# One body and a loop in place of seven nested bodies for the extra units of an expert layer

## The chip, the cores and the metric

The kernel runs on one core of one Trainium2 chip. The metric is device time in microseconds (us) of one execution, smaller being better; the median of several runs is compared.

## The reference, cut to what matters

An encoder of two layers over 256 tokens of width 1024. Each layer mixes tokens and then applies a mixture of 32 experts in 4 groups of 8: a token takes the group with the largest logit and in it the two experts with the largest logits.

```python
for g in range(N_EXPERT_GROUPS):
    h = jax.nn.silu(jnp.einsum('nd,edf->enf', xt, w_gate[g])) * jnp.einsum('nd,edf->enf', xt, w_up[g])
    h = h * gate[:, g].T[:, :, None].astype(h.dtype)
    y = y + jnp.einsum('enf,efd->nd', h, w_down[g])
```

`gate` is zero for all experts but a token's two. How many tokens an expert gets is known only at run time.

## The kernel before, in words

The kernel streams all weights of all 32 experts of a layer from HBM (3 MB an expert, in pages of 1 MB) through a ring of 25 pages in on-chip memory. The list of pages (`chunks`) has a fixed order; `pump` (L227) issues transfers on SyncE's queue (SP) as long as the plan says that pages are free, and each `done` and `work_done` calls it again.

`moe` (L1194) goes over the experts of a layer in nine blocks of two or four (`ORDER`). A block of four has 32 slots for an expert, one of two has 64. For a block the tokens of its experts are gathered by matmuls with a one-hot matrix (`gather`, L1232), multiplied with the gate and up weights (`gate_up`, L1442), made hidden values (`hidden`, L1345, and `hidden_t`, L1351), multiplied with the down weights (`down`, L1458), split into a high and a low part (`split_y`, L1359) and added to x (`combine`, L1251 to L1253). `fill_slots` (L1335) makes the matrix that takes slots back to tokens, by two transposes, a copy on ScalarE (L1341) and a compare on VectorE (L1342); it writes into `scr`, a work page of the ring that each block takes anew.

Where an expert of a block of four has more than 32 tokens, `second` (L1480) does the block once more for the next 32; it stands within a test (`tc.If`, L1559 and L1589). Where an expert has more than 64 tokens, each further 128 are a unit. `unit_list` (L1300) makes the list of units on VectorE: in `uw["ui"]` the expert of each unit, up to 7 (`MAXU`), and in place 14 their number; `uw["ub"]` holds the experts and the first slots as numbers on every partition. `unit_prepare` (L1374), in block 3 of layer 0 and block 4 of layer 1, takes work pages for a unit's weights and issues the five transfers of unit 0 (`unit_load`, L1366: two of gate, two of up, one of down), each with the condition that there is a unit at all.

After block 3 of layer 0 and block 5 of layer 1 (`UNIT_AT`), `unit_chain` (L1423) runs: a test for unit 0, within it the body of unit 0 and a test for unit 1, within that the loads and the body of unit 1, and so on to unit 6. A unit (`unit`, L1381) is some 25 instructions on VectorE, matmuls at L1398, L1411 and L1419, transposes, and a `combine`. Every engine makes the tests by itself, from the number of units that it reads into a register at L1606. After the units `work_done(6, 4)` gives six pages back to the ring: three of weights, one of tokens, `scr` and the block's `y`.

The framework puts each engine's instructions in order, assigns the semaphores of engines and transfers, and adds the semaphore instructions of a test that fails.

Of the kernel before, what the change touches and what calls it, by code (L numbers as in the profile page):

```python
# [14 lines left out]
I32 = mybir.dt.int32  # L15
# [43 lines left out]
MAXU = 7  # L59
# [102 lines left out]
def hybrid_encoder_kernel(ctx, tc, I, out, dbg=None):  # L162
    nc = tc.nc
    V, S, G, PE = nc.vector, nc.scalar, nc.gpsimd, nc.tensor
# [5 lines left out]
    def ps(name):  # L170
        return psp.tile([128, 512], F32, tag="ps", name=name)
# [97 lines left out]
    def work_done(n, peak=None):  # L269
        st["nw"] -= n  # L270
        if peak is not None:
            st["peak"] = peak
        pump()
# [89 lines left out]
    def either(dst, src, scale=None):  # L363

        flip[0] ^= 1
        st["bits"], st["picked"] = "SV"[flip[0]], 0
        copy(dst, src, scale)
# [3 lines left out]
    def transpose(dst, src):  # L371
        PE.transpose(dst, src, ident[:src.shape[0], :src.shape[0]])  # L372
# [4 lines left out]
    def page_sm(t, o, shape):  # L377
        n = int(np.prod(shape))
        v = t[:, o:o + n]
        if len(shape) == 2:  # L380
            v = v.rearrange("p (a b) -> p a b", a=shape[0])
        elif len(shape) == 3:
            v = v.rearrange("p (a b c) -> p a b c", a=shape[0], b=shape[1])
        return v
# [809 lines left out]
    def moe(l, tab, rt):  # L1194
        with tc.tile_pool(name=f"moe{l}", bufs=1, reuse_waits="tile") as mo:
            vc = vec[:, l, :]

            def mt(shape, name, dt=F32, tag=None, bufs=1):
                return mo.tile(shape, dt, tag=tag or name, name=name, bufs=bufs)
# [45 lines left out]
            def combine(pend, hfs=(0, 1)):  # L1245
                Sm, yh, yl = pend
                for hf in hfs:
                    for tt in range(2):
                        p = ps("cp")
                        c = slice(512 * hf, 512 * hf + 512)  # L1250
                        PE.matmul(p, Sm[:, 128 * tt:128 * tt + 128], yh[:, c], start=True, stop=False)  # L1251
                        PE.matmul(p, Sm[:, 128 * tt:128 * tt + 128], yl[:, c], start=False, stop=True)  # L1252
                        V.tensor_tensor(x[:, tt, c], p, x[:, tt, c], OP.add)  # L1253
# [76 lines left out]
            def slots(blocks, tag=""):  # L1330

                n = 1 if tag else 2
                return (mt([128, T], "sm" + tag, F32R, bufs=n), mt([128, 1], "gs" + tag, bufs=n)), blocks

            def fill_slots(arg):  # L1335
                (Sm, gs), blocks = arg
                p = ps("slp")
                for tt in range(2):
                    transpose(p[:, 128 * tt:128 * tt + 128], blocks[tt])
                gj = scr[0][:, 1024:1280]  # L1340
                S.activation(gj, p[:, :T], AF.Copy, accum_out=gs)  # L1341
                V.tensor_scalar(Sm, p[:, :T], 0.0, None, op0=OP.is_gt)  # L1342
                return Sm, gs

            def hidden(gu, gs):  # L1345
                sl, hh = scr[0][:, 1280:1536], scr[0][:, 1536:1792]
                S.activation(sl, gu[:, 0:256], AF.Silu)  # L1347
                V.scalar_tensor_tensor(hh, gu[:, 256:512], gs, sl, op0=OP.mult, op1=OP.mult)  # L1348
                return hh

            def hidden_t(hh, o=1792):  # L1351
                hp = ps("hp")
                for j in range(2):
                    transpose(hp[:, 128 * j:128 * j + 128], hh.rearrange("p (f j) -> p j f", j=2)[:, j, :])
                hT = page_sm(scr[0], o, (2, 128))
                S.copy(hT.rearrange("p a b -> p (a b)"), hp[:, :256])
                return hT

            def split_y(yp, yh, yl, c):  # L1359
                S.copy(yh[:, c], yp)  # L1360
                V.tensor_tensor(yl[:, c], yp, yh[:, c].bitcast(F32), OP.subtract)  # L1361


            uw = {}

            def unit_load(u, **kw):  # L1366
                e = nc.sync.value_load(uw["ui"][0:1, u:u + 1], min_val=0, max_val=NE - 1)
                for h in range(2):
                    for a, n in enumerate(("w_gate", "w_up")):
                        nc.sync.dma_start(uw["gu"][h][:, a], I[n][l][ds(e, 1)].rearrange(  # L1370
                            "a (p k) f -> p (a k) f", k=8)[:, 4 * h:4 * h + 4, :], **kw)
                nc.sync.dma_start(uw["dn"], I["w_down"][l][ds(e, 1)].rearrange("a (p j) d -> p (a j) d", j=2), **kw)
# [8 lines left out]
            def unit(u):  # L1381
                ub = uw["ub"]
                oh, rs_, jk = mt([128, NE], "ohu"), mt([128, 4], "rsu"), mt([128, NE], "jku")
                V.tensor_scalar(oh, io32, ub[:, u:u + 1], None, op0=OP.is_equal)
                for tt in range(2):
                    V.tensor_tensor_reduce(jk, rk[:, tt, :], oh, 1.0, 0.0, OP.mult, OP.add, rs_[:, tt:tt + 1])
                    V.tensor_tensor_reduce(jk, gate[:, tt, :], oh, 1.0, 0.0, OP.mult, OP.add, rs_[:, 2 + tt:3 + tt])
                V.tensor_scalar(rs_[:, 0:2], rs_[:, 0:2], ub[:, MAXU + u:MAXU + u + 1], None, op0=OP.subtract)
                Pu, Pg = mt([128, 2, 128], "Pu", tag="oh"), page_sm(scr[0], 1536, (2, 128))
                for tt in range(2):  # L1390
                    V.tensor_scalar(Pu[:, tt], iota, rs_[:, tt:tt + 1], None, op0=OP.is_equal)
                    V.tensor_scalar(Pg[:, tt], iota, rs_[:, tt:tt + 1], rs_[:, 2 + tt:3 + tt], op0=OP.is_equal,
                                    op1=OP.mult)
                xu, xuT = uw["xu"][:, :D], page_sm(uw["xu"], D, (8, 128))
                for hf in range(2):
                    p = ps("gpu")
                    for tt in range(2):
                        PE.matmul(p, Pu[:, tt], xn[:, tt, 4 * hf:4 * hf + 4, :].rearrange("p k d -> p (k d)"),  # L1398
                                  start=(tt == 0), stop=(tt == 1))
                    either(xu[:, 512 * hf:512 * hf + 512], p)  # L1400
                for hf in range(2):
                    p = ps("xup")
                    for k in range(4):
                        transpose(p[:, 128 * k:128 * k + 128], xu[:, 128 * (4 * hf + k):128 * (4 * hf + k) + 128])
                    V.tensor_tensor(xuT[:, 4 * hf:4 * hf + 4, :], p.rearrange("p (k s) -> p k s", k=4),
                                    vc[:, V_LN2 + 4 * hf:V_LN2 + 4 * hf + 4].unsqueeze(2).to_broadcast([128, 4, 128]),
                                    OP.mult)
                Sm, gs = fill_slots(slots([Pg[:, 0], Pg[:, 1]]))
                gu = ps("guu")
                for k in range(8):  # L1410
                    PE.matmul(gu.rearrange("p (a f) -> p a f", a=2), xuT[:, k], uw["gu"][k // 4][:, :, k % 4, :],  # L1411
                              start=(k == 0), stop=(k == 7))
                hT = hidden_t(hidden(gu, gs))
                yh, yl = uw["y"]
                for hf in range(2):
                    c = slice(512 * hf, 512 * hf + 512)
                    yp = ps("ypu")
                    for j in range(2):
                        PE.matmul(yp, hT[:, j, :], uw["dn"][:, j, c], start=(j == 0), stop=(j == 1))  # L1419
                    split_y(yp, yh, yl, c)  # L1420
                combine((Sm, yh, yl))

            def unit_chain(nu, u):  # L1423
                with tc.If(nu > u):  # L1424
                    if u:
                        unit_load(u)
                    unit(u)
                    if u + 1 < MAXU:
                        unit_chain(nu, u + 1)

            def gate_up(gu, blk, xs, hf, ahead=None):

# [72 lines left out]
            for g, grp in enumerate(groups):  # L1505
# [3 lines left out]
                for ib, b in enumerate(grp):  # L1509
# [92 lines left out]
                    if b == UNIT_AT[l]:  # L1602
                        combine(pend)
                        pend = None
                        n = 2 * MAXU
                        unit_chain(nc.values_load(uw["ui"][0:1, n:n + 1], min_val=0, max_val=MAXU), 0)  # L1606
                        work_done(6, 4)
                    if b >= TAB_AT and tab is not None:
                        next(tab, None)
# [54 lines left out]
    for l in range(L):  # L1664
        rt = mixer(l)
        if dbg and dbg.get("stop") == ("mixer", l):
            break
        moe(l, follow(l + 1, TABLES.split(), s5_steps(l + 1), STATE) if l + 1 < L else None, rt)
        if dbg and dbg.get("stop") in (("moe", l), ("blk", l)):
            break  # L1670
# [26 lines left out]
```

## Time and profile before

| | us |
|---|---|
| median of 3 runs | 740.88 (740.05 to 741.61) |
| the profiled execution | 737.13 |
| its span, first to last instruction | 735.4 |
| mean granted TensorE clock, share of full speed | 0.955 |

The profile is of one execution. Its engines are PE (TensorE's matmuls), PEld (its weight loads), DVE (VectorE), ACT (ScalarE), POOL (GpSimd) and SP (SyncE, which only issues transfers here). A q behind an engine's name marks an instruction of its sequencer: branches, semaphore instructions, issues of transfers. `L1442` is a line of the kernel. `out<-in` are names of tiles: `pg` is a page of weights, `gu` the result of gate and up, `slp` the transposed slots, `scr` the work page.

### The profile page before, as it was taken

The page shows a single profiled execution, that of the slowest core. Times are in us where ns is not written, and L with a number is a line of the kernel's source. Part 1 is how long each engine was busy: PE and PEld are TensorE (multiplying, and loading weights), DVE is VectorE, ACT ScalarE, POOL GpSimd, SP SyncE. Part 2 cuts the span into 40 slices and gives each one's busy share as a digit, 9 for nine tenths or more (in the row PEclk, how much of TensorE's full clock was granted, in tenths as well). Part 3 has the DMA queues.
Part 4 walks back from the last instruction along what each step waited for, and adds up shares of the span by engine and source line. Part 5 has one row for each costly group of instructions (what it writes and reads, how often), then busy time and mean ns, then how long its engine had stood idle before and what let it go on. Part 6 is the DMA issues. An engine that isn't in the chain of part 4 may idle for free. (4 is left out here: it accounts for less than half of the span.)

```text
span 735.4 us, 12004 instructions
## 1 busy us (share of the span) xinstructions
PE 631.6 (86%) x4370; PEld 386.3 (53%) x4370; DVE 373.7 (51%) x899; ACT 253.2 (34%) x578; POOL 107.5 (15%) x135
## 2 busy tenths in 40 slices
PE   7997989889799498598799899989899987769994
PEld 6584877744245334336268677775444434324442
DVE  3899977532334117824279878752423324322424
ACT  3647873421012014524074397352111211001113
POOL 1202001000000021521051754510000000000001
PEclk9999999999899799889999999989999999979998
DMA  8920375896999899999994715895999999998992
GB/s 304 419 108 0 117 289 215 331 389 231 413 406 416 280 405 411 412 415 407 398 417 183 286 59 172 302 362 194 333 416 406 392 410 413 416 366 301 410 382 83
DMA packets 57207, 232.90 MB, mean 317 GB/s; under 512 B 6048, under 2 KB 8480, under 8 KB 48160
## 3 DMA queue, kind: packets, MB, share of 16 engines
q1 hardware_dynamic: 57120, 231.75, 81.5%
q8 instruction: 53, 0.87, 0.5%
q14 instruction: 34, 0.28, 0.1%
HBM read 233.82 MB, written 1.05 MB: 319 GB/s over the span
## 5 line engine op out<-in xcount | busy, mean ns | idle before, releaser
L1442 PE MATMUL gu<-pg,xe 128*32 128x512 f32 (+1 forms) x1024 | 147.9, 618 | 12.4 <-DMA pg<-in_w_up_dram 7.1
L1458 PE MATMUL yp<-pg,scr 128*32 128x512 f32 (+2 forms) x560 | 79.4, 639 | 25.9 <-DVEq L1589 11.5
L1442 PEld LDWEIGHTS gu<-pg,xe 128*32 128x32 f32 (+1 forms) x1024 | 48.1, 117 | 96.7 <-issue 91.0
L1236 PE MATMUL gp<-oh,xn 128*128 128x128 f32 (+1 forms) x416 | 71.2, 325 | 4.0 <-DVE oh L1221 2.0
L1236 PEld LDWEIGHTS gp<-oh,xn 128*128 128x128 f32 x416 | 61.4, 197 | 18.6 <-issue 10.6
L1458 PEld LDWEIGHTS yp<-pg,scr 128*32 128x32 f32 (+1 forms) x560 | 22.1, 120 | 73.0 <-issue 58.2
L1361 DVE TENSOR_TENSOR y<-yp,y 128x512 fp32r<-128x512 f32 (+1 forms) x39 | 26.3, 677 | 65.8 <-ACT y L1360 65.8
L1348 DVE SCALAR_TENSOR_TENSOR scr<-gu,gs,scr 128x256 f32<-128x256 f32 x19 | 9.1, 481 | 97.1 <-ACT scr L1347 97.1
L1228 POOL TENSOR_TENSOR pgt<-oh,gate 128x256 f32<-128x256 f32 (+1 forms) x13 | 10.2, 783 | 316.5 <-PE slp L372 304.6
L1253 DVE TENSOR_TENSOR x<-cp,x 128x512 f32<-128x512 f32 x76 | 48.9, 685 | 14.2 <-PE cp L1252 14.2
L1360 ACT CAST y<-yp 128x512 fp32r<-128x512 f32 (+1 forms) x39 | 22.3, 575 | 88.1 <-PE yp L1458 86.6
L359 DVE TENSOR_SCALAR xe<-gp,vec 128x128 f32<-128x128 f32 (+1 forms) x52 | 20.8, 400 | 52.0 <-PE gp L1236 52.0
L355 ACT ACTIVATE xe<-gp,vec 128x128 f32<-128x128 f32 (+1 forms) x52 | 21.3, 409 | 73.3 <-PE gp L1236 73.2
L1347 ACT ACTIVATE scr<-gu 128x256 f32<-128x256 f32 x19 | 7.3, 384 | 102.3 <-PEq L1559 52.3
L1251 PE MATMUL cp<-y,sm 128*128 128x512 f32 x76 | 34.0, 455 | 0.3 <-PEq L1559 0.2
L1252 PE MATMUL cp<-y,sm 128*128 128x512 f32 x76 | 30.4, 409 | 1.5 <-DVE y L1361 1.5
L1058 DVE SCALAR_TENSOR_TENSOR x<-op,rg,x 128x512 f32<-128x512 f32 x24 | 17.9, 749 | 16.8 <-PE op L681 11.9
L1341 ACT ACTIVATE scr<-slp 128x256 f32<-128x256 f32 x20 | 7.8, 388 | 42.2 <-SPq L1424 28.8
L1251 PEld LDWEIGHTS cp<-y,sm 128*128 128x128 f32 x76 | 14.5, 192 | 10.4 <-issue 8.2
L372 PE MATMUL hp<-cst,scr 128*128 128x128 f32 x40 | 9.3, 314 | 12.2 <-DVE scr L1348 11.1
L372 PE MATMUL slp<-cst,pgt 128*128 128x128 f32 x36 | 8.3, 314 | 11.2 <-DVEq L1424 5.9
L1252 PEld LDWEIGHTS cp<-y,sm 128*128 128x128 f32 x76 | 14.3, 193 | 5.5 <-DVE y L1361 3.8
(454 smaller groups left out, 1209.2 us busy)
## 6 DMA issues: line engine op xcount, KB each, us to landing
pg<-in_w_gate_dram SPq DMA_DIRECT2D x128, 512.0 KB, 10.1
pg<-in_w_up_dram SPq DMA_DIRECT2D x128, 512.0 KB, 10.4
pg<-in_w_down_dram SPq DMA_DIRECT2D x56, 1024.0 KB, 11.8
pg<-in_w_o_dram SPq DMA_DIRECT2D x8, 1024.0 KB, 18.0
pg<-in_w_down_dram SPq DMA_DIRECT2D x12, 512.0 KB, 10.4
pg<-in_w_qk_dram SPq DMA_DIRECT2D x4, 1024.0 KB, 14.9
pg<-in_w_nat_dram SPq DMA_DIRECT2D x4, 960.0 KB, 12.8
wgu<-in_w_gate_dram SPq DMA_DIRECT2D x4, 512.0 KB
```

The source lines that it names most:

```text
L355: S.copy(dst, src) if scale is None else S.activation(dst, src, AF.Copy, scale=scale)
L359: e.tensor_scalar(dst, src, scale, None, op0=OP.mult)
L372: PE.transpose(dst, src, ident[:src.shape[0], :src.shape[0]])
L1058: V.scalar_tensor_tensor(xh, p, rg[:, g, tt:tt + 1], xh, op0=OP.mult, op1=OP.add)
L1236: PE.matmul(p[:, :w], xn[:, tt, k, :], P[:, tt].rearrange("p e c -> p (e c)"), start=(tt == 0), stop=(tt == 1))
L1251: PE.matmul(p, Sm[:, 128 * tt:128 * tt + 128], yh[:, c], start=True, stop=False)
L1252: PE.matmul(p, Sm[:, 128 * tt:128 * tt + 128], yl[:, c], start=False, stop=True)
L1253: V.tensor_tensor(x[:, tt, c], p, x[:, tt, c], OP.add)
L1360: S.copy(yh[:, c], yp)
L1361: V.tensor_tensor(yl[:, c], yp, yh[:, c].bitcast(F32), OP.subtract)
L1442: PE.matmul(gu[m * s:m * s + m, :].rearrange("p (a f) -> p a f", a=2), xs(k, s), page(l, "gu", e, hf)[:, :, k % 4, :], start=(k == 0), sto ...
L1458: PE.matmul(yp[m * s:m * s + m, :], hT[:, j, m * s:m * s + m], page(l, "dn", e)[:, j, c], start=(j == 0), stop=(j == 1), tile_position=(0, ...
```

## The change

`units` takes the place of `unit_chain`. Unit 0 has its body within the first test, as before. Within a test for a second unit stands a loop over units 1 to the last. Its body moves the lists of units down by one place on VectorE (six copies in all), loads the weights of what is now unit 0, and runs the body for unit 0.

```diff
-            def unit_chain(nu, u):
-                with tc.If(nu > u):
-                    if u:
-                        unit_load(u)
-                    unit(u)
-                    if u + 1 < MAXU:
-                        unit_chain(nu, u + 1)
+            def units(nu):
+
+                with tc.If(nu > 0):
+                    unit(0)
+                    with tc.If(nu > 1):
+                        with tc.For_i(1, nu, 1):
+                            ui, ub = uw["ui"], uw["ub"]
+                            for a in (0, MAXU):
+                                mv = mt([128, MAXU], "umv")
+                                V.tensor_copy(mv[:, :MAXU - 1], ub[:, a + 1:a + MAXU])
+                                V.tensor_copy(ub[:, a:a + MAXU - 1], mv[:, :MAXU - 1])
+                            mi = mt([1, MAXU], "umi", I32)
+                            V.tensor_copy(mi[:, :MAXU - 1], ui[:, 1:MAXU])
+                            V.tensor_copy(ui[:, :MAXU - 1], mi[:, :MAXU - 1])
+                            unit_load(0)
+                            unit(0)
...
-                        unit_chain(nc.values_load(uw["ui"][0:1, n:n + 1], min_val=0, max_val=MAXU), 0)
+                        units(nc.values_load(uw["ui"][0:1, n:n + 1], min_val=0, max_val=MAXU))
```

## Rows read from the trace of the kernel before

**Rows 1.** The page: its span, and the transfer rate in 40 equal slices.

```profile
span 735.4 us, 12004 instructions
...
GB/s 304 419 108 0 117 289 215 331 389 231 413 406 416 280 405 411 412 415 407 398 417 183 286 59 172 302 362 194 333 416 406 392 410 413 416 366 301 410 382 83
```

**Rows 2.** Stretches: PE, PEld, DVE, ACT, POOL busy us (instructions), clock, DMA share, GB/s.

```profile
241.00:252.00 11.00, 3.18 (x15) 2.07 (x19) 1.12 (x2) 0.48 (x2) 0.00 (x0) 0.59 0.69 219
252.00:259.00 7.00, 6.60 (x56) 4.15 (x48) 0.00 (x0) 0.27 (x1) 0.00 (x0) 0.91 1.01 346
259.00:350.00 91.00, 74.64 (x720) 39.01 (x724) 46.95 (x111) 34.99 (x68) 21.82 (x22) 0.94 1.02 412
...
657.00:664.00 7.00, 6.94 (x54) 1.85 (x45) 0.49 (x2) 0.47 (x2) 0.00 (x0) 0.82 0.44 173
664.00:673.00 9.00, 9.00 (x80) 5.44 (x84) 2.89 (x6) 1.12 (x4) 0.00 (x0) 1.00 0.91 272
```

**Rows 3.** SP's waits from 250 to 390: who <- whom, us, times, longest.

```profile
SPq L247 <- DMA pg<-in_w_down_dram: 29.3, 19, 2.2
```

**Rows 4.** Issues of transfers: times issued, KB each, median us to landing.

```profile
pg<-in_w_gate_dram SPq DMA_DIRECT2D x128, 512.0 KB, 10.1
```

**Rows 5.** Timeline at layer 0's units: start, us, instruction, [idle before <- releaser].

```profile
239.75 0.07 SPq L1372 DMA_DIRECT2D wdn<-in_w_down_dram  x1
...
243.45 0.33 SPq L247 DMA_DIRECT2D pg<-in_w_gate_dram  x1
...
244.48 0.66 PE L372 MATMUL slp<-cst,pgt 128*128 128x128 f32 x2 [5.29 <-PEq L1424]
...
248.90 0.33 SPq L247 DMA_DIRECT2D pg<-in_w_up_dram  x1
248.97 0.38 ACT L1341 ACTIVATE scr<-slp 128x256 f32<-128x256 f32 x1 [11.51 <-SPq L1424]
...
249.48 9.11 PE L1442 MATMUL gu<-pg,xe 128*32 128x512 f32 x64 [4.34 <-issue]
```

**Rows 6.** SP's waits from 243 to 249.3.

```profile
SPq L1424 <- SPq L1424: 4.6, 4, 2.7
```

**Rows 7.** The units' test: count, ns min/median/max, first to last start.

```profile
L1424 SPq EVENT_SEMAPHORE  x18: 17/17/17, 244.3 to 662.8; - x18
...
L1424 PEldq COMPARE_BRANCH  x4: 70/2794/6028, 238.7 to 653.1; - x4
```

**Rows 8.** Timeline at layer 1's units.

```profile
646.61 0.33 SPq L247 DMA_DIRECT2D pg<-in_w_gate_dram  x1
...
651.63 0.33 SPq L247 DMA_DIRECT2D pg<-in_w_up_dram  x1
...
653.59 0.66 PE L372 MATMUL slp<-cst,pgt 128*128 128x128 f32 x2 [5.95 <-DVEq L1424]
...
654.18 9.71 PE L1442 MATMUL gu<-pg,xe 128*32 128x512 f32 x64
...
662.97 0.39 ACT L1341 ACTIVATE scr<-slp 128x256 f32<-128x256 f32 x1 [17.24 <-SPq L1424]
...
663.61 0.34 SPq L247 DMA_DIRECT2D pg<-in_w_gate_dram  x1
```

**Rows 9.** SP's waits from 652 to 663.2.

```profile
SPq L1424 <- SPq L1424: 10.1, 5, 5.2
```

**Rows 10.** A unit's matmuls with gate and up: count, ns, first to last start.

```profile
L1411 PE MATMUL guu<-wgu,xu x16: 592/592/595, 632.4 to 638.8; 128*128 128x512 f32 x16
```

**Rows 11.** The one unit's stretch, columns as in rows 2.

```profile
624.20:647.70 23.50, 18.49 (x54) 8.60 (x52) 9.23 (x27) 2.99 (x7) 0.00 (x0) 1.00 1.02 415
```

**Rows 12.** The later test of `second`, on TensorE's queue.

```profile
L1589 PEldq COMPARE_BRANCH  x15: 78/318/1681, 182.8 to 717.5; - x15
```

**Rows 13.** Timeline of TensorE in the last two blocks: gate and up.

```profile
689.69 5.33 PE L1442 MATMUL gu<-pg,xe 128*32 128x512 f32 x48
...
707.56 8.78 PE L1442 MATMUL gu<-pg,xe 128*32 128x512 f32 x62 [0.30 <-PEq L1559]
```

## The prediction

> **What bounds the kernel now.** I read the page's slices first. In both expert stretches the transfer rate lies at 405 to 418 GB/s, slice after slice, and it falls in three slices there: the fourteenth (280), the thirty-sixth (366) and the thirty-seventh (301) [rows 1]. Finer stretches place the dips exactly: 219 and 346 GB/s from 241 to 259 us, 173 and 272 GB/s from 657 to 673 us, with 412 after the first [rows 2]. These are the two places where the extra units stand, block 3 of layer 0 and block 5 of layer 1. The waits of the queue that issues transfers say what a dip costs: between 250 and 390 us SyncE (SP) mostly waits for earlier transfers to land [rows 3], so the expert stretches are bound by weight traffic, and bytes not moved in a dip are time. At 412 GB/s the first dip is short by 11 x 193 + 7 x 66 = 2585 KB, 6.3 us, the second by 7 x 239 + 9 x 140 = 2933 KB, 7.1 us. So 13.4 us is the most that these two places can give.
>
> Next, who leaves the transfer queue empty. A 512 KB page takes 10.1 us from issue to landing [rows 4]; at 412 GB/s that is 4.2 MB, eight pages in flight. In layer 0 SP issues a page at 243.45 us and the next at 248.90 us [rows 5]. Between the two stands the skip of the units: nine semaphore instructions in each of two skips (18 of them), one of SP's own and, as I read it, one for each of the eight transfers that can be in flight [rows 7]. A body that is skipped must leave each semaphore as if it had run, so each of the nine waits for what is under way on its semaphore and then adds what the body would have added. The waits bear this out: 4 of them, 4.6 us, in layer 0 [rows 6]; 5 of them, 10.1 us, in layer 1, of which 5.2 is one [rows 9]. The other four of layer 1 come to 4.9 us, 1.2 each, and a page at 412 GB/s is 1.27 us: they end with the landings of the last four pages issued. SP therefore drains its whole queue before it issues again, at 663.61 us, 12.0 us after its last page [rows 8].
>
> TensorE stands still at the same places: 5.3 us and then 4.3 us with no semaphore to wait for in layer 0 [rows 5], 5.95 us in layer 1 [rows 8]. Its branch at the units' test took up to 6.0 us, with a median of 2.8 [rows 7], while at the test of `second` it took 0.3 us in the median [rows 12]. By the code the latter jumps over 74 matmuls and as many loads; a unit is 54 and 52 [rows 11], so the long ones jump over six or seven times 106 instructions.
>
> How many units run: the body's gate-and-up matmuls are there once, 16 records between 632 and 639 us [rows 10]. So layer 0 has none and layer 1 has one, and the loop's body is not entered in either layer.
>
> **The change part by part.** Unit 0 stays as it was: same instructions, same test, nothing to price. The six copies on VectorE, the register loop and the loop's own loads lie inside the test for a second unit, which fails: nothing. What is left is what the skipped code looks like.
>
> (a) The transfers in it. Nested, six `unit_load`s hold 30 transfers and touch all eight semaphores. The loop holds one, 5 transfers, and if the semaphores go on being used in turn, these are the five oldest. In layer 0 they belong to the five loads of 233 to 239.75 us, which carry no bytes as there is no unit, so the wait ends at once: SP is through the test at 244.9 instead of 248.9 us, 4.0 us earlier (the 4.6 us of [rows 6], less some 0.6 for the jump and six semaphore instructions). In layer 1 the youngest of the five is the fourth last page, issued at 646.61 us; the waits for the three after it go: 3 x 1.23 = 3.7 us, and SP is through at 659.2 instead of 662.9 us. The single 5.2 us wait is SP's own jump [rows 9]; gone or not, it ends at 657.7 us, before that landing. Bounds of (a): nothing, if all eight are still waited for; 13.4 us, if the dips vanish.
>
> (b) The jumps. In layer 1 TensorE's jump shrinks from six bodies to one of some 106 instructions plus the loop's ends, which is less than `second` has, so 0.3 us for 5.95. In layer 0 it is two bodies, some 230 instructions, between the 148 of `second` and the 740 of now: 0.3 to 5.4 us; I take the middle, 2.9. First the row: with a jump over 636 or 742 instructions the branch takes 5 to 6 us, over 148 it takes 0.3 [rows 7, 11, 12]. [...]
>
> What (b) is worth: in layer 0 TensorE has slack, busy 74.6 of the next 91 us while the transfers run at 412 GB/s [rows 2]; so nothing, or up to 1 us through the 346 GB/s stretch, if pages come free late there. In layer 1 the next block's gate and up (9.7 us from 654.18) end at 663.9, and ScalarE is let go at 662.97 [rows 8]: both halves of that chain end together now, so both have to move. With (b) the matmuls end near 656, and the block's further work starts with SP's 659.2, 3.7 us earlier. Without (b) only 0.3 us would be won there. TensorE then idles some 4 us before it, and an idle of 5.3 us was followed by a granted clock of 0.59 [rows 2, 5]; a few us of half speed cost 2 us at most, and the last block's gate and up hold 1.9 us of waiting for pages (62 matmuls in 8.78 us, where 48 took 5.33) [rows 13], which earlier transfers give back. I take nothing for it and keep 2 us for the range.
>
> (c) Moved code. Later jumps land elsewhere in the instruction stream; one such branch took 1.7 us [rows 12]. I take nothing, plus or minus 1.
>
> Sum: 4.0 + 3.7 = 7.7 us. Layer 0's part passes through to the end, since every later stage only starts earlier. The profiled execution took 737.13 us (span 735.4) and becomes 729.4; the median of the runs shown, 740.88, becomes 733.2. What a measurement of this kernel can tell from no change is about 0.2%, 1.5 us.
>
> **The rivals.**
> *All eight are still waited for*, because a loop is closed by a wait for every transfer or because the loop's five fall on the youngest. For it: nothing in the trace shows a loop. Against: waits on all eight are what 30 transfers taken in turn would leave, and 5 in turn would leave five [rows 7, 9]. Then only TensorE's lateness goes: 1 us in layer 0, 0.3 in layer 1, so 739.5 us. Chance 0.13.
> *Only one layer pays.* In layer 1 TensorE is busy for all of 664 to 673 us [rows 2]; if its clock falls or its jump still misses, 3.7 us shrinks to 0 to 1. Then 736.5 us. Chance 0.12.
> *Slower: the engines meet at the skipped loop.* If the loop makes all engines wait there for SP's drained queue, the 9.7 us of matmuls that run in layer 1 before 662.9 us come behind it: they would end at 672.6 rather than 663.9, 8.7 us later, with 0 in layer 0, where they start at 249.5 anyway. That gives 749.6 us. It decides once the meeting ends later than the present 654, by more than what (a) gives. For it: each engine has a share in the skip already. Against: now each passes it by itself (TensorE's test stands at 238.7 us, SP's semaphores at 244.3) [rows 7]. Chance 0.11.
> *The jumps are the bound.* TensorE's idle time at the units, 5.3 + 4.3 + 5.95 = 15.5 us, less 0.9 for three short jumps, would all come back: 726.3 us. [...] Against it: 13.4 us is all that the transfers have lost. Chance 0.04.
>
> **How the numbers follow.** The forecast has 0.60: 733.2 us, by itself 730 to 736. The range must leave out no more than 0.2. I let it run from 728.5 to 741: inside lie the forecast with 2 us for the clock and 1 for moved code, the one-layer case and the unchanged wait; outside lie the slower case (0.11) and most of the jump case. Faster by over 0.2% are the forecast, the one-layer case, the jump case and a little of the unchanged wait: 0.78. Same: the rest of that wait, 0.11. Slower: 0.11.
>
> **What the changed profile would show.** SP's semaphore instructions at the units: six in each skip, not nine. Its first page after them near 245 us in layer 0, 1.5 us after the page before it, and in layer 1 within 9 us of the last one, with no stretch at 0 GB/s. TensorE's branch in layer 1 under 1 us. ScalarE's slot copy after the units idle for 7 to 8 us in layer 0, not 11.5. I am wrong if nine semaphores stay, if TensorE or ScalarE wait for SP before the next block's matmuls, or if the dips close and the end doesn't move, which would mean that TensorE sets it.

## The result, and the profile after

The changed kernel took 730.87 us in the median of four runs (727.9 to 735.1), the kernel before 740.46 beside it: ratio 0.9885, 95% interval 0.9849 to 0.9921. Two further measurements of it, told below, gave 0.9872 and 0.9888. That is 8.3 to 9.5 us of some 740; the sum had 7.7, and 733.2 us. One of the six executions of the first of these (run 1) took 838.39 us at a granted clock of 0.73; its ratio leaves it out, its median of 730.8 us does not (730.23 without it).

The two profiled executions differ by less, 737.13 and 735.1 us. The profiled one of after is the slowest of its four runs, and it is late before any changed instruction: SP issues the last page ahead of layer 0's unit loads at 235.62 us where before it did so at 230.78. So the two traces have to be compared by stretches that start at the same page, not by their clocks from the start.

The page first: its span, the transfer rate in 40 slices, and the issues of a 512 KB page with the median time to landing [rows 1, 4].

```profile
span 733.3 us, 12000 instructions
...
GB/s 309 419 105 0 118 275 177 329 386 200 409 410 416 307 416 407 414 414 409 396 417 251 286 59 142 261 363 267 241 414 408 413 408 415 412 410 358 408 380 71
...
pg<-in_w_gate_dram SPq DMA_DIRECT2D x128, 512.0 KB, 10.2
```

Layer 0's dip is in the fourteenth slice still (307 for 280), layer 1's is one slice of 358 where there were two of 366 and 301. Finer, in stretches laid around the same places [rows 2] (columns: busy us and instructions of PE, PEld, DVE, ACT, POOL, granted clock, DMA share, GB/s):

```profile
245.00:250.00 5.00, 4.42 (x38) 1.40 (x36) 0.30 (x2) 0.47 (x2) 0.00 (x0) 1.00 0.73 235
250.00:252.00 2.00, 2.00 (x27) 0.68 (x19) 0.26 (x1) 0.00 (x0) 0.00 (x0) 1.00 0.91 250
252.00:263.00 11.00, 9.40 (x85) 2.87 (x80) 2.29 (x4) 2.30 (x6) 3.36 (x3) 1.00 1.00 358
...
657.00:664.00 7.00, 6.76 (x64) 4.12 (x57) 1.08 (x3) 0.47 (x2) 0.00 (x0) 1.00 0.91 346
664.00:673.00 9.00, 9.00 (x82) 3.69 (x80) 2.30 (x5) 1.27 (x4) 0.00 (x0) 1.00 1.02 338
```

Against 412 GB/s the first dip is now short by 5 x 177 + 2 x 162 + 11 x 54 = 1803 KB, 4.4 us (6.3 before), the second by 7 x 66 + 9 x 74 = 1128 KB, 2.7 us (7.1 before). TensorE's granted clock is 1.00 in all five, where it was 0.59 after layer 0's units; in layer 1 it was lower only ahead of them (0.66 from 652 to 657 us).

The semaphore instructions and branches of the two tests (L1425 the first unit, L1427 the second; count, ns min/median/max, first to last start) [rows 7]:

```profile
L1425 SPq EVENT_SEMAPHORE  x6: 17/17/17, 248.8 to 249.2; - x6
...
L1425 PEldq COMPARE_BRANCH  x2: 70/197/324, 242.3 to 625.9; - x2
...
L1427 SPq EVENT_SEMAPHORE  x6: 17/17/17, 655.1 to 660.5; - x6
...
L1427 PEldq COMPARE_BRANCH  x2: 180/258/336, 650.3 to 651.2; - x2
```

Six semaphore instructions a skip in place of nine. TensorE's branch takes 0.32 us in layer 0 and 0.34 in layer 1, where it took 5.4 and 6.0.

The timeline at both places (start, us, instruction, [idle before <- releaser]) [rows 5, 8]:

```profile
244.41 0.41 PE L372 MATMUL slp<-cst,pgt 128*128 128x128 f32 x2 [1.57 <-DVEq L1425]
...
248.26 0.33 SPq L247 DMA_DIRECT2D pg<-in_w_gate_dram  x1
...
249.32 0.33 SPq L247 DMA_DIRECT2D pg<-in_w_up_dram  x1
...
653.85 0.33 SPq L247 DMA_DIRECT2D pg<-in_w_up_dram  x1
...
660.63 0.38 ACT L1341 ACTIVATE scr<-slp 128x256 f32<-128x256 f32 x1 [11.56 <-DMA pg<-in_w_gate_dram]
...
661.08 0.34 SPq L247 DMA_DIRECT2D pg<-in_w_gate_dram  x1
```

In layer 0 SP issues the page after the test 1.06 us after the page ahead of it (5.45 before), so it waits for nothing there. In layer 1 the gap is 7.2 us (12.0 before), and its waits at the test from 651 to 661 us have come down to two [rows 9]:

```profile
SPq L1427 <- SPq L1427: 5.5, 2, 5.1
```

The longer one ends with a landing, that of a gate page, as ScalarE's releaser names it; SP issued one at 648.82, the fourth last before the test.

**Two stretches by which all kernels are compared.** The pages have one order in all of them (357 issues). Layer 0: from the 100th page, the last ahead of the unit's loads, to the 161st. Layer 1: from the 319th page, the last ahead of the units' test, to the end of the span. Before, then after:

```profile
230.78 0.33 SPq L247 DMA_DIRECT2D pg<-in_w_up_dram  x1
...
333.14 0.33 SPq L247 DMA_DIRECT2D pg<-in_w_gate_dram  x1
```

```profile
235.62 0.33 SPq L247 DMA_DIRECT2D pg<-in_w_up_dram  x1
...
334.52 0.33 SPq L247 DMA_DIRECT2D pg<-in_w_gate_dram  x1
```

Layer 0: 102.4 us before, 98.9 after. Layer 1: 735.4 - 651.63 = 83.8 before [rows 8], 733.3 - 653.85 = 79.5 after.

**One moment decides layer 1's stretch.** Behind the units the next block needs `second`, whose first matmuls gather its tokens (`gpa`). They come behind the block's own gate and up on TensorE, and they need `scr`, which waits for SP's way through the test. The start of `gpa`, and the last `yp` matmuls, before and then after:

```profile
663.96 3.84 PE L1474 MATMUL gpa<-scr,xn 128*128 128x128 f32 x32
...
724.04 1.07 PE L1458 MATMUL yp<-pg,scr 128*32 128x256 f32 x16
```

```profile
661.71 3.81 PE L1483 MATMUL gpa<-scr,xn 128*128 128x128 f32 x32 [0.24 <-DVE scr L1495]
...
721.76 1.07 PE L1467 MATMUL yp<-pg,scr 128*32 128x256 f32 x16
```

From the one to the end of the other pass 61.1 to 61.5 us in all thirteen traces of this document, whatever the pages do meanwhile. So from `gpa` on TensorE sets the end, before the change as after it, and what the change is worth in layer 1 is how much earlier `gpa` starts, counted from the 319th page: 12.3 us before (13.2 in run 5, which has the nested bodies there), 7.9 after (8.1 to 8.4 in runs 1, 6 and 9).

### The profile page after: what moved, and what is told of

It is laid out like the page before. It is cut to its first block, busy times and chain, and to the rows that moved or that the text cites. A ratio compares the mean times of both kernels' runs of the same rounds, so it can differ in the third digit from the quotient of the medians.

```text
span 733.3 us, 12000 instructions
## 1 busy us (share of the span) xinstructions
PE 639.2 (87%) x4370; PEld 389.2 (53%) x4370; DVE 373.2 (51%) x899; ACT 252.9 (34%) x578; POOL 107.4 (15%) x135
## 3 DMA queue, kind: packets, MB, share of 16 engines
q1 hardware_dynamic: 57120, 231.75, 81.3%
## 5 line engine op out<-in xcount | busy, mean ns | idle before, releaser
L1451 PE MATMUL gu<-pg,xe 128*32 128x512 f32 (+1 forms) x1024 | 149.5, 619 | 11.4 <-DMA pg<-in_w_up_dram 9.9
L1467 PE MATMUL yp<-pg,scr 128*32 128x512 f32 (+2 forms) x560 | 77.9, 628 | 26.1 <-DVEq L1598 12.8
L1451 PEld LDWEIGHTS gu<-pg,xe 128*32 128x32 f32 (+1 forms) x1024 | 45.9, 117 | 98.8 <-issue 94.5
L1236 PE MATMUL gp<-oh,xn 128*128 128x128 f32 (+1 forms) x416 | 73.6, 331 | 3.9 <-DVE oh L1221 1.6
L1236 PEld LDWEIGHTS gp<-oh,xn 128*128 128x128 f32 x416 | 62.9, 201 | 19.0 <-issue 11.3
L1251 PEld LDWEIGHTS cp<-y,sm 128*128 128x128 f32 x76 | 14.3, 189 | 10.4 <-issue 8.2
L548 PE MATMUL t4p<-ca,tabs 128*32 128x32 f32 (+3 forms) x512 | 16.3, 250 | 2.1 <-issue 2.1
L548 PEld LDWEIGHTS t4p<-ca,tabs 128*32 128x32 f32 x512 | 15.4, 116 | 3.3 <-issue 3.0
```

The lines of the kernel that those rows point to most:

```text
L548: PE.matmul(t4p[b][32 * jq:32 * jq + 32, c + lo:c + hi], g0[ri][:, 8 * d + i, :], ca[ri][:, 8 * d + i, m, :].rearrange("p m c -> p (m c)") ...
L1236: PE.matmul(p[:, :w], xn[:, tt, k, :], P[:, tt].rearrange("p e c -> p (e c)"), start=(tt == 0), stop=(tt == 1))
L1451: PE.matmul(gu[m * s:m * s + m, :].rearrange("p (a f) -> p a f", a=2), xs(k, s), page(l, "gu", e, hf)[:, :, k % 4, :], start=(k == 0), sto ...
L1467: PE.matmul(yp[m * s:m * s + m, :], hT[:, j, m * s:m * s + m], page(l, "dn", e)[:, j, c], start=(j == 0), stop=(j == 1), tile_position=(0, ...
```

## The experiments

All runs beside the kernel before on the same chip; the stretches are read from each run's own trace as above. Runs 1 to 4 shared a chip, as did 5 to 8 and 9 to 11. The ratio is not the quotient of the two medians beside it; they differ by up to 0.24%. What is given in us by a ratio is the ratio's difference from 1 times the median of before. A trace shows one execution, so a stretch is one reading.

| | ratio (95%) | median, before | layer 0 us | layer 1 us |
|---|---|---|---|---|
| before | | | 102.4 | 83.8 |
| after | 0.9885 (0.9849 to 0.9921) | 730.87, 740.46 | 98.9 | 79.5 |
| 1 after again | 0.9872 (0.9823 to 0.9921) | 730.8, 741.91 | 100.0 | 80.0 |
| 2 two bodies, no loop | 0.9862 (0.9808 to 0.9917) | 731.45, 741.91 | 99.2 | 81.2 |
| 3 seven bodies, five loads | 0.9933 (0.9902 to 0.9964) | 736.57, 741.91 | 100.3 | 84.6 |
| 4 loop, ten loads | 0.9979 (0.9949 to 1.0009) | 738.89, 741.91 | 101.4 | 83.2 |
| 5 loop in layer 0 only | 0.9951 (0.9921 to 0.998) | 735.99, 738.54 | 98.6 | 84.5 |
| 6 loop in layer 1 only | 0.9909 (0.9875 to 0.9943) | 731.69, 738.54 | 103.1 | 79.4 |
| 7 loop without loads | 0.9892 (0.9841 to 0.9943) | 732.29, 738.54 | 99.1 | 79.1 |
| 8 three loads a unit | 0.9856 (0.9817 to 0.9896) | 729.67, 738.54 | 97.5 | 80.4 |
| 9 after, third time | 0.9888 (0.9853 to 0.9922) | 729.51, 738.26 | 99.4 | 79.7 |
| 10 three loads again | 0.9879 (0.984 to 0.9918) | 729.16, 738.26 | 96.6 | 78.9 |
| 11 no empty loads | 0.9846 (0.9807 to 0.9884) | 727.12, 738.26 | 96.4 | 78.4 |

The same code read again differs by up to 1.4 us in layer 0 (98.6 to 100.0 with the loop) and 0.7 us in layer 1 (83.8 and 84.5 with the nested bodies).

**1, 9. The changed kernel again.** No edit.

> The changed kernel once more, to place the others beside it on one chip. Both theories: 0.985 to 0.992 of the kernel before, some 731 us beside 740.5.

> The changed kernel a third time, beside the two below on one chip: ratio 0.987 to the kernel before. From the page before the unit's loads in layer 0 to the 41st page after them 66 to 67 us, as in the earlier traces of it (before: 69.5).

0.9872 and 0.9888, as the first time. The stretch that run 9 was to repeat (from the 100th page to the 140th) was 66.5 us.

**2. Two nested bodies, no loop.**

```diff
-                        with tc.For_i(1, nu, 1):
...
-                            unit_load(0)
-                            unit(0)
+                        unit_load(1)
+                        unit(1)
```

> Two nested bodies and no loop: unit 0, and within its test unit 1 with its five loads; units 2 to 6 are left out (these inputs have at most one unit in a layer). The skipped code holds five transfers, as with the loop, and one body less its copies. If the gain comes from what the skipped code holds (its transfers, or its length), the time is that of the changed kernel within 0.2%, some 731 us. If the loop itself gives or costs something (a meeting of the engines, code that lies elsewhere), it differs by more: by 1 us or more either way.

0.9862 and 731.45 us, 0.65 us from run 1: no difference that can be told (its layer 1 reads 1.6 us longer than the loop's, its layer 0 the same). The loop's form neither gives nor costs anything here, and the engines do not meet at it.

**3. Seven nested bodies, loads in the second alone: long jumps, five transfers.**

```diff
             def units(nu, u=0):
                 with tc.If(nu > u):
-                    if u:
+                    if u == 1:
                         unit_load(u)
```

> Seven nested bodies as before, but only unit 1 has loads; the loads of units 2 to 6 are left out (no unit of these inputs needs them). So the jumps stay long and the skipped code holds five transfers. Theory A, the transfer queue waits for what the skipped code would have moved: SP is free 4.0 us earlier in layer 0 (near 245), and in layer 1 near 659, but there TensorE's matmuls still end near 664, so only 0.3 us is won; 4.3 us in all, 736.2 us, ratio 0.994. Theory B, the long jumps of the engines are what costs: nothing is won, 740.5 us, ratio 1.000, though SP's semaphore instructions go from nine to six.

0.9933 for 0.994, and not 1.000. The tests of this kernel, on SP and on TensorE:

```profile
L1424 SPq EVENT_SEMAPHORE  x12: 17/17/17, 246.4 to 659.9; - x12
...
L1424 PEldq COMPARE_BRANCH  x4: 70/3130/6105, 239.5 to 654.7; - x4
```

Six a skip, with jumps as long as before: what fell away is the waiting for transfers alone. Layer 0 is 2.4 us shorter than the nested mean of 102.7 (102.4 and 103.1); layer 1 (84.6) has gained nothing, in this one trace. Its timeline says why:

```profile
659.98 0.38 ACT L1341 ACTIVATE scr<-slp 128x256 f32<-128x256 f32 x1 [12.82 <-SPq L1424]
...
660.45 0.33 SPq L247 DMA_DIRECT2D pg<-in_w_gate_dram  x1
...
664.42 0.82 PE L1474 MATMUL gpa<-scr,xn 128*128 128x128 f32 x5
```

SP and ScalarE are free near 660, 9.0 us after SP's last page (12.0 before), but TensorE came out of its jump 6 us late and gets to the next matmuls, `gpa`, at 664.42, 13.0 us after the 319th page (12.3 in before and 13.2 in run 5). What SP won is lost there.

**4. The loop with its loads twice: short jumps, all eight semaphores.**

```diff
-                            unit_load(0)
+                            for _ in range(2):
+                                unit_load(0)
```

> The changed kernel with the loop's five loads issued twice, so ten transfers that touch all eight semaphores; the jumps stay short. Theory A: nine semaphore instructions a skip again, SP near 249 in layer 0 and near 663 in layer 1; only TensorE's earlier branch is left, 1.3 us at most, 739.2 us, ratio 0.998. Theory B: as the changed kernel, 731 us, ratio 0.987.

0.9979 for 0.998, and not 0.987. Nine semaphore instructions a skip are back, with TensorE's branches at 0.3 us:

```profile
L1425 SPq EVENT_SEMAPHORE  x9: 17/17/17, 247.4 to 252.0; - x9
...
L1427 SPq EVENT_SEMAPHORE  x9: 17/17/17, 654.1 to 663.4; - x9
```

In layer 1 TensorE now ends its gate and up early and waits: 1.21 us of idle time ahead of the next matmuls, which end with SP's drained queue.

```profile
663.50 0.38 ACT L1341 ACTIVATE scr<-slp 128x256 f32<-128x256 f32 x1 [12.48 <-PE gu L1452]
...
664.09 0.33 SPq L247 DMA_DIRECT2D pg<-in_w_gate_dram  x1
...
664.58 0.68 PE L1484 MATMUL gpa<-scr,xn 128*128 128x128 f32 x4 [1.21 <-DVE scr L1496]
```

The trace names the matmuls as ScalarE's releaser; SP's last semaphore instruction stands at 663.4, and the copy itself needs only the transposed slots of 654.2, so I read SP's drain as what ended that wait. `gpa` starts 11.4 us after the 319th page.

Runs 3 and 4 with before and after make a table of two by two, in us of the stretches (nested: mean of before and of the runs 5 or 6 that leave that layer nested; loop: mean of the traces of after and of runs 1, 9 and 5 or 6):

| | layer 0, long jumps | layer 0, short | layer 1, long jumps | layer 1, short |
|---|---|---|---|---|
| all eight semaphores | 102.7 | 101.4 | 84.1 | 83.2 |
| five transfers | 100.3 | 99.2 | 84.6 | 79.6 |

In layer 1 either alone is worth next to nothing (-0.5 and 0.9), and both are worth 4.5: `gpa` starts when the later of TensorE and SP is through. In layer 0 the readings are 2.4 and 1.3, and 3.5 together, but 1.3 is within the 1.4 us by which the same code differs. What the transfers moved in the 60 us from the 100th page on tells the two apart better. Before, then runs 4, 3 and after (columns as above):

```profile
230.78:290.78 60.00, 47.36 (x311) 24.10 (x312) 20.85 (x66) 13.30 (x27) 3.68 (x3) 0.91 0.96 369
...
234.20:294.20 60.00, 49.60 (x306) 19.85 (x304) 27.24 (x76) 14.09 (x30) 7.69 (x10) 0.97 0.93 363
...
232.96:292.96 60.00, 48.10 (x307) 20.47 (x305) 22.50 (x70) 12.98 (x26) 4.77 (x6) 0.91 1.00 385
...
235.62:295.62 60.00, 48.84 (x310) 19.84 (x308) 28.23 (x77) 15.10 (x31) 8.60 (x11) 0.99 0.99 380
```

The same 60 us give 364 GB/s in run 6, whose layer 0 is nested, and 389 to 391 in runs 1, 5 and 9. So in layer 0 the transfers in the skipped code make the difference, 363 to 369 against 380 to 391, and the short jumps alone bring the transfers nothing that can be seen.

**5, 6. One layer alone.**

```diff
             def units(nu):
+                if l != 0:          # run 5; run 6 has 1
+                    return unit_chain(nu, 0)
...
```

Below it `unit_chain` stands as it did before.

> One body and the loop in layer 0, the seven nested bodies in layer 1. If both layers pay as the sum has it, 4.0 us of transfers and up to 1 of the jump: 736 us, ratio 0.994. If one layer alone carries the gain: 0.987 here and 1.000 with layer 1 alone, or the other way round.

> The seven nested bodies in layer 0, one body and the loop in layer 1. If both layers pay: 3.7 us, 737 us, ratio 0.995; and this run's gain and that of layer 0 alone add up to that of the whole change (0.987). SP's first page after the units within 9 us of the last in layer 1, 5.4 us after it in layer 0.

0.9951 and 0.9909: both layers pay. In us that is 3.6 and 6.7, with intervals of about 2.2 and 2.5 either way; together 10.3, beside 8.3 to 9.5 for both. The traces give 3.5 and 4.5 (the table above), which is within both intervals.

**7. The loop without loads.**

```diff
                                 V.tensor_copy(ui[:, :MAXU - 1], mi[:, :MAXU - 1])
-                            unit_load(0)
                             unit(0)
```

> The changed kernel without the loads in the loop's body (no unit of these inputs needs them), so the skipped code holds no transfer at all. If SP's remaining wait in layer 1, for the landing of the fourth last page, still costs, it goes: SP is free some 5 us earlier there, and of the 2.7 us that the transfers still lose at this place up to all come back, 728 to 729 us, ratio 0.983. Layer 0 gives nothing, since SP no longer waits there. Rival: TensorE's matmuls or the pages that come free set the end at this place by now, and the time is that of the changed kernel, 731 us, 0.987.

Layer 1's dip is gone, and layer 0's is not (columns as above):

```profile
245.00:250.00 5.00, 4.42 (x37) 1.33 (x40) 0.84 (x2) 0.47 (x2) 0.00 (x0) 1.00 0.78 261
250.00:255.00 5.00, 3.90 (x33) 1.08 (x26) 0.48 (x1) 0.38 (x1) 0.00 (x0) 1.00 0.93 263
...
657.00:664.00 7.00, 7.00 (x65) 4.82 (x60) 1.62 (x3) 0.66 (x3) 0.00 (x0) 1.00 1.02 410
664.00:673.00 9.00, 7.44 (x68) 2.37 (x64) 1.40 (x4) 1.32 (x4) 0.00 (x0) 1.00 1.03 419
```

Yet the ratio is 0.9892 and layer 1's stretch 79.1 us for 79.6: of the 2.7 us of transfers some 0.5 reach the end, less than the 0.7 by which readings differ there. The expected 728 to 729 us did not come, and the rival was right: TensorE is busy for all of 657 to 664 us, and `gpa` starts 7.6 us after the 319th page, at the end of the block's gate and up, though SP issues its next page 1.5 us after it.

**8, 10. Three loads a unit in place of five.** Gate whole into one page, up whole into the other.

```diff
-                for h in range(2):
-                    for a, n in enumerate(("w_gate", "w_up")):
-                        nc.sync.dma_start(uw["gu"][h][:, a], I[n][l][ds(e, 1)].rearrange(
-                            "a (p k) f -> p (a k) f", k=8)[:, 4 * h:4 * h + 4, :], **kw)
+                for a, n in enumerate(("w_gate", "w_up")):
+                    nc.sync.dma_start(uw["gu"][a], I[n][l][ds(e, 1)].rearrange("a (p k) f -> p (a k) f", k=8), **kw)
...
```

The shape of the two pages and the unit's gate and up, 16 matmuls in place of 8, change with it.

> The changed kernel with three loads a unit in place of five: gate whole into one page, up whole into the other (1 MB each), down as before, and the unit's gate and up as 16 matmuls of 256 columns in place of 8 of 512. All of the reference is computed. In layer 0 three transfers without bytes in place of five: the dip of some 4.4 us shrinks to about three fifths, 1.5 us won. In layer 1 SP waits for the landing of the sixth last page, 2.5 us earlier, of which up to 2 are won; the 8 matmuls more cost under 0.5 us. 728 us, ratio 0.983. Rival: what is left of the dips comes from the restart of the transfers and not from the number of loads, and the time is that of the changed kernel, 731 us, 0.987.

> The kernel with three loads a unit again. By the trace of its first run layer 0 is 1.8 us shorter than with five loads (64.1 us in place of 66 to the 41st page) and layer 1 the same: ratio 0.9845 if that reaches the end, 0.987 if TensorE takes it back.

In the trace layer 0 is 2.1 us shorter than with five loads, both times (97.5 and 96.6, mean 97.1, against 99.2); layer 1 is as it was (80.4 and 78.9). The ratios, 0.9856 and 0.9879, beside 0.9872 to 0.9888 for the changed kernel, do not tell the two apart: on the one chip where both ran they are 729.16 and 729.51 us. Faster than before it is; that it beats the changed kernel is not shown.

These two kernels have one difference more. TensorE's test in layer 0 stalls again, though it skips two bodies only, as in the changed kernel, each longer by eight matmuls and their loads (run 8; 6.0 us in run 10, 0.32 in after):

```profile
L1424 PEldq COMPARE_BRANCH  x2: 70/3070/6071, 242.4 to 623.2; - x2
```

The transfers moved 402 and 407 GB/s all the same in the 60 us from the 100th page. So the stall did not grow with the code that was jumped over: 6.1 us over two such bodies (run 8), 5.4 over seven and 6.0 over six (before). In layer 0 it did not hold up the transfers.

**11. No loads of unit 0 in layer 0 either.** Run 7, and there:

```diff
-                unit_load(0, cond=n > 0, cond_hint=False)
+                if l:
+                    unit_load(0, cond=n > 0, cond_hint=False)
+                else:
+                    for t in (uw["gu"][0][:, 0, 0], uw["gu"][1][:, 0, 0], uw["dn"][:, 0]):
+                        nc.gpsimd.memset(t[:, :1], 0.0)
```

> The loop without loads, and in layer 0 no loads of unit 0 either, in place of the five that carry no bytes (layer 0 has no unit in these inputs; three memsets of one column on GpSimd stand in for them). If each empty load holds one of eight places in flight, the dip that is left in layer 0 (some 3.6 us with the loop without loads) goes, as layer 1's did: no stretch under 390 GB/s from 240 to 262 us, 728 us, ratio 0.983 to 0.985. If it comes from the restart and not from the empty loads, the dip stays and the time is that of the loop without loads.

```profile
245.00:250.00 5.00, 3.69 (x36) 1.37 (x39) 0.00 (x0) 0.00 (x0) 0.00 (x0) 1.00 1.02 406
250.00:255.00 5.00, 3.34 (x27) 1.07 (x23) 0.48 (x1) 0.76 (x2) 0.00 (x0) 0.98 1.03 406
```

The dip of 261 and 263 GB/s is gone, layer 0's stretch is 96.4 us for run 7's 99.1, and the time is the least of all, 727.12 us, ratio 0.9846 (its interval overlaps that of run 7). So what was left of the dip in layer 0 comes from the loads that carry no bytes.

## Why the prediction was right, point by point

**The transfers in the skipped code (4.0 and 3.7 us).** Right in mechanism: six semaphore instructions for nine, no wait in layer 0, one landing to wait for in layer 1, that of the fourth last page as forecast. In size, transfers and jumps together gave 3.5 us in layer 0 and 4.5 in layer 1 by the traces, 8.0 for a sum of 7.7; run 3, with the transfers' part alone, gave 2.4 in layer 0. The ground that the text gives, that both stretches are bound by weight traffic, holds in layer 0 and not in layer 1: there TensorE sets the end from `gpa` on, and the 3.7 us were right because SP's way through the test is also what `scr` waits for.

**The jumps in layer 1.** "Both halves of that chain end together now, so both have to move" held: run 3 moved SP alone and won nothing, run 4 moved TensorE alone and won 0.9, where 0.3 was put to each. What did not come is the room that the text saw on TensorE: matmuls that end "near 656", and then "some 4 us" idle. Its own figures give 663.9 - 5.65 = 658.2; in after they ended 7.6 us after the 319th page, 659.3 on the clock of before, and TensorE idled 0.24 us (1.35 in run 1). The two halves end together still, and so run 7 found nothing more to win there. The 2 us kept for a falling clock were hardly needed: it fell ahead of the place, to 0.66 from 652 to 657 us, in the profiled execution of after, and not in that of run 1 (1.00 from 646 to 668), and the stretches of the two, 79.5 and 80.0 us, do not show it.

**The jumps in layer 0 ("nothing, or up to 1 us").** The runs do not contradict this, and do not settle the size. Run 4 has the jumps' part alone; its stretch is 1.3 us shorter, within the scatter, and its transfers move no more. SP's waits from 249 to 268 us show how a late TensorE reaches the transfers. Before, then run 3:

```profile
SPq L247 <- PEq L1559: 5.0, 1, 5.0
```

```profile
SPq L247 <- PEq L1559: 4.0, 1, 4.0
```

SP waits for pages that TensorE gives back at the test of `second` behind the block. In the same stretch of after and of run 4, whose jumps are short, SP has no wait for TensorE. But run 3 moves 385 GB/s with this wait, where the loop without it moves 380 to 391, so that the wait costs the end anything is not shown. The length of the jump was taken too long, 2.9 us for the measured 0.32, and as growing with the code that is skipped, which runs 8 and 10 do not bear out (6.1 and 6.0 us over two bodies); nothing hung on it.

**What the sum left out in layer 0.** The five loads without bytes stand in the text only as waits that end at once. Both kernels issue them, so the sum, a difference, does not need them; with the drain gone they are what is left of the dip, 2.7 us of the stretch (run 7 against run 11).

**Moved code (plus or minus 1).** Run 2, whose skipped code is shorter by the loop's ends and copies, so that what follows lies elsewhere again, is 0.65 us from run 1.

**The rivals.** "All eight are still waited for" was priced at 739.5 us; run 4, which has just that, has 0.9979, which makes 739.3 of 740.88. "Only one layer pays": run 5 and run 6 both pay. "Slower: the engines meet": no meeting; TensorE and VectorE pass the second test in layer 1 by 652.3 us while SP waits there until 660.5. "The jumps are the bound": run 4 has the short jumps alone and is 1.6 us faster by its ratio (3.8 at most by its interval), where this rival had 14.6; run 3 keeps the long ones and is 5.0 faster. The jump itself did shrink (6.0 us over six bodies, 0.34 over one with the loop); as far as the runs show, the time hung on it in layer 1 alone, and there only where transfers were let go too.

**What was to be seen.** All of it, with one shift: SP's first page after the units was forecast near 245 us and stands at 249.32, in an execution 4.84 us late by then. ScalarE's slot copy in layer 0 was to idle 7 to 8 us, and idles 8.24:

```profile
249.33 0.38 ACT L1341 ACTIVATE scr<-slp 128x256 f32<-128x256 f32 x1 [8.24 <-SPq L1425]
```

One reading of the text is loose, and nothing hangs on it: two slices of the expert stretches stand at 398 and 392 GB/s, outside its "405 to 418" [rows 1].

**What stays open.** Run 3 measured 5.0 us (2.7 to 7.3 by its interval), where the two stretches of its trace give 1.9; that it won nothing in layer 1 rests on that one execution and on the 61 us from `gpa` on that all traces share. Run 6 measured 6.7 us where the traces give 4.5; its interval holds both. Whether short jumps alone are worth anything in layer 0, and whether three loads beat five, is not settled by the runs. Why TensorE's branch takes 0.32 us over two bodies and 6 us over two that are a little longer is not tested.

## What to carry to other kernels

A body that a test skipped still cost its queue. With 30 transfers in the skipped code, or with 10, SP passed nine semaphore instructions a skip and waited 10.1 and 9.2 us at layer 1's test (before, run 4); with 5 it passed six and waited 5.5 us (after); with none its trace shows no wait there (run 7). So what counts is how many transfers stand in the body that is not run, up to eight as I read the nine, and not how often it runs. Where SP's drain and a long jump of TensorE ended together, shortening one was worth next to nothing (-0.5 and 0.9 us in layer 1), and both 4.5 us; read both ends before pricing either, and look for the instruction that waits for both, here `gpa`. A jump's stall has to be read from a trace of the kernel as it will be: it was 0.3 us or some 6, and with bodies longer by eight matmuls (runs 8 and 10) it was back. Conditional transfers that moved nothing were not free either (2.7 us for five, run 7 against run 11); issue as few of them as the layout allows.

## What was not expected of the hardware

Five transfers without bytes (all issues of before come to 234.9 MB with layer 0's five counted at full size, and its queue moved 231.75, so those 3.1 MB were not moved) cost layer 0 2.7 us (run 7 against run 11); three cost 0.7 (mean of runs 8 and 10 against run 11), which is within the scatter. How they do it is not shown. My guess is that they hold places that pages would have had; their issues, which come 1.1 to 2.4 us apart like those of pages (237.53 to 243.89 us in run 7), and the dip that follows them would fit that, but no run changes the number of places. Behind a gap in SP's issues the transfers came back slowly: from 664 to 673 us of before, right behind the first page at 663.61, the DMA engines are busy 0.91 of the time and move 272 GB/s [rows 2]; in after, behind a shorter gap, 1.02 goes with 338; in run 7, without a gap, 1.03 goes with 419.
